# Two tiles instead of one between a head pair's projection and its turn into q and k, with one more tile of lead

## The chip, the core and the metric

The kernel runs on one core of one Trainium2 chip. The metric is the device time of one launch in microseconds (us), as the median of several runs. Four compute engines matter here: TensorE (PE, matrix products and transposes into PSUM), VectorE (DVE), ScalarE (ACT) and GpSimd (POOL). SyncE (SP) issues nearly all DMA transfers. Each engine takes its instructions in the order in which they were written into its own queue, and waits where an operand or a buffer is not ready.

## The reference

One block of a hybrid decoder, on a sequence of 2048 tokens of width 1024. The input is normalised (RMS), scaled and shifted by a conditioning vector, and multiplied by one matrix whose columns feed three mixers: A, a chunked gMLP with four groups of 64 columns; B, an mLSTM with four heads of 96; C, a stick-breaking attention with six heads of 64. The gated outputs are joined, projected, and added to the input. The change touches C alone:

```
q, k = rms_norm(q, g_q), rms_norm(k, g_k)          # over each head's 64 columns
for blk in range(S // 128):                        # 128 queries, all keys up to them
    z = (q_blk @ k^T) * 64 ** -0.5
    beta = sigmoid(z), 0 where key >= query        # strictly causal
    # a key's weight is beta there, times the product of (1 - beta) over
    # the keys between it and the query
    att = beta * reversed exclusive cumprod(1 - beta)
    out_blk = att @ v
```

## The kernel before

The 2048 tokens are 16 tiles of 128, worked on in three blocks of 5, 5 and 6 tiles (`BLOCKS`). Within a block the normalised, modulated input lies transposed in SBUF (`hT`), split into a coarse and a fine part; each projection is three matrix products for each of eight slices of the inner dimension, 24 matrix products for a tile (L297 to L299; `pc` is the projection of C, `pv`, `pb` and `pg` of B, `pa` of A). They go into a PSUM pool of three buffers, `pproj`.

The attention C runs in each block as three stages, one for each pair of heads (`p` = 0, 1, 2). For each tile of the pair, `c_proj` makes q, k and v, and `c_evac` takes them from PSUM in two parts. Part one (L351 to L362): ScalarE squares, VectorE sums (L353), GpSimd takes the power -1/2 (L354, L355), v is copied, and VectorE writes the normalised `qk` (L360), which is the last reader of the PSUM buffer. Part two, behind the `yield`, is the turning: four PE transposes `pq` (L366), two ACT copies (L369, L370), two VectorE operations into `Kst` (L371) and `Qst` (L373), and in blocks 0 and 1 two DMAs that keep k and v for later blocks.

The attention itself, `stick`, is a software pipeline of units (a tile, a head, up to four key tiles): products `z` (L401, L402), two sigmoids on ACT (L406, L407), a scan on VectorE (L414), a multiplication (L418) that goes by turns to VectorE and GpSimd, transposes `at` on PE (L429), ACT and VectorE splitting them into `aT` (L431, L432), and the products `av` (L444). A query tile ends with L448, L450 and two small products `py` (L460). `interleave` mixes these units by cost with a side stream: the rest of the pair's projection and then other projections as fillers, wrapped by `behind`.

`need` lets an attention unit of tile j start only once `ready` has reached j, which `evac_finish` sets when a tile's turning has been written. `lead` says how many tiles of the pair's projection are written ahead of the attention. The last stage of a block runs beside a short filler list, and then comes the tail: the projection `pv` of the block, into which the next block's input is mixed. `get_x` loads a tile, VectorE scales it (L149), GpSimd adds the shift (L150), and `hT_half` transposes it (L289) into a `pproj` buffer and splits it (ACT L290, VectorE L291).

All of this is the order in which the program is written. A list scheduler with priorities then places each engine's instructions, so what is written earlier in the text is a priority and not yet the order of a queue.

Of the kernel before, what the change touches and what calls it, by code (L numbers as in the profile page):

```python
# [33 lines left out]
def hybrid_block_kernel(ctx: ExitStack, tc: tile.TileContext, x, c, norm_g, w_ada, b_ada, w_in,  # L34
# [120 lines left out]
    def get_x(i, j):  # L155
        load_x(i, j % 2)
        rms_x(i)
        for hh in range(len(xtiles[i][0])):
            w = D // len(xtiles[i][0])
            mod_x(i, hh * w, (hh + 1) * w)  # L160
# [158 lines left out]
    pend = []  # L319
# [1 line left out]
    ready = [-1]  # L321

    def evac_finish():
        j, e = pend.pop()
        run(e)
        ready[0] = j

    def evac_later(e, j):

        next(e)  # L330
        if pend:
            evac_finish()
        pend.append((j, e))

    def behind(cp, rest):

        yield from cp
        for m, c in enumerate(rest):
            if m == 6 and pend:
                evac_finish()  # L340
            yield c
        if pend:
            evac_finish()

    def c_evac(b, t0, p, j, ps):
# [126 lines left out]
    def stick_cost(t0, nb):  # L472
        return sum(2 * ((i + 1) * (2 * P / 2.4 + 218) + 215) for i in range(t0, t0 + nb))
# [47 lines left out]
    def bg_proj(t0, nb, half):  # L521
        c0 = half * 192
        with prio(HIGH[0]):
            wt = weights(w_in[0], [(OFF["bo"] + c0, 192), (OFF["bz"] + c0, 192)])
        for j in range(nb):
            i = t0 + j
            ps = pproj.tile([P, 512], F32, tag="proj", name=f"pg{half}_{i}")
            yield from proj_tc(ps[:, :384], wt, j, 384)
            sg = t512(f"sgg{half}_{i}")
            nc.scalar.activation(sg[:, 0:384], ps[:, 0:384], AF.Sigmoid)  # L530
            g = t512(f"gg{half}_{i}")
            nc.vector.tensor_tensor(g[:, 0:192], ps[:, 192:384], sg[:, 192:384], ALU.mult)
            nc.gpsimd.tensor_tensor(sg[:, 0:192], sg[:, 0:192], hn_bc[:, c0:c0 + 192], ALU.mult)
            nc.gpsimd.tensor_tensor(g[:, 0:192], g[:, 0:192], sg[:, 0:192], ALU.mult)
            nc.sync.dma_start(gate_d[i * P:(i + 1) * P, c0:c0 + 192], g[:, 0:192])

    def cz_proj(t0, nb):
        with prio(HIGH[0]):
            wt = weights(w_in[0], [(OFF["cz"], 384)])
        for j in range(nb):  # L540
            i = t0 + j
            ps = pproj.tile([P, 512], F32, tag="proj", name=f"pcz{i}")
            yield from proj_tc(ps[:, :384], wt, j, 384)
            sg = t512(f"sgz{i}")
            nc.scalar.activation(sg[:, 0:384], ps[:, 0:384], AF.Sigmoid)
            nc.vector.tensor_tensor(sg[:, 0:384], ps[:, 0:384], sg[:, 0:384], ALU.mult)
            nc.sync.dma_start(gate_d[i * P:(i + 1) * P, 384:768], sg[:, 0:384])
# [181 lines left out]
    def gate_gemv():  # L729
        acc = tmp.tile([P, D], F32, tag="xt", name="gacc")  # L730
        for n in range(2):
            cs = slice(n * 512, (n + 1) * 512)
            for k in range(KT):
                st = stg_p.tile([P, 2, WMAX], F32, tag="st", name=f"stgate{n}_{k}").rearrange("p a f -> p (a f)")
                nc.sync.dma_start(st[:, 0:512], w_ada[0, k * P:(k + 1) * P, 2048 + n * 512:2560 + n * 512])
                if k == 0:
                    nc.vector.tensor_scalar(acc[:, cs], st[:, 0:512], c_act[:, 0:1], None, ALU.mult)
                else:
                    nc.vector.scalar_tensor_tensor(acc[:, cs], st[:, 0:512], c_act[:, k:k + 1], acc[:, cs],
                                                   ALU.mult, ALU.add)  # L740
                yield 0
            pg = pproj.tile([P, 512], F32, tag="proj", name=f"pgt{n}")
            nc.tensor.matmul(pg[0:1, :], lhsT=ones_sq[:, 0:1], rhs=acc[:, cs], start=True, stop=True)
            gr = t512(f"gate{n}")
            nc.sync.dma_start(gr[0:1, :], b_ada[:, 2048 + n * 512:2560 + n * 512])
            nc.vector.tensor_tensor(gr[0:1, :], pg[0:1, :], gr[0:1, :], ALU.add)
            nc.sync.dma_start(ga_d[:, cs], gr[0:1, :])
            yield 860

    def run(g):  # L750
        for _ in g:
            pass

    def chain(*gens):
        for g in gens:
            yield from g

    def mix(a, n, g):
        for m, c in enumerate(a):
            yield c  # L760
            if m % n == n - 1:
                yield next(g, 0)
        yield from g
# [75 lines left out]
    for b, nb in enumerate(BLOCKS):  # L839
        last = b == len(BLOCKS) - 1  # L840
        chunk = nb * KT * 3 * 384 / 2.4
        HIGH[0] = 0 if b == 0 else -4000
        fillers = [
            (chain(bqk_proj(t0, nb, 0), bqk_proj(t0, nb, 1), bg_proj(t0, nb, 0)), 3),
            (chain(bg_proj(t0, nb, 1), cz_proj(t0, nb), a_proj(t0, nb, 0)), 3),
            (a_proj(t0, nb, 1), 1),
        ]
        if b == 1:
            fillers[0] = (mix(fillers[0][0], 8, gate_gemv()), 3)
        if last:  # L850
            fillers[0] = (mix(fillers[0][0], 36, gating()), 3)
            fillers[1] = (mix(fillers[1][0], 14, first_chunk()), 3)
        for p in range(3):
            lead = min(nb, 2 + b)
            if p > 0:
                ready[0] = -1
                cp = c_proj(b, t0, nb, p)
                for _ in range(lead * KT + 1):
                    next(cp)
            cp_cost = 0 if b == 0 and p == 0 else (nb - lead) * KT * 3 * 384 / 2.4  # L860
            if b == 0 and p == 0:
                HIGH[0] = -400
            if p == 2 and not last:
                get_x(t0 + nb, 0)
                get_x(t0 + nb + 1, 1)
            interleave(stick(p, t0, nb), stick_cost(t0, nb), behind(cp, fillers[p][0]), cp_cost + fillers[p][1] * chunk)
        tail = bv_proj(t0, nb)
        if last:
            run(tail)
        else:  # L870
            t1, n1 = t0 + nb, BLOCKS[b + 1]
            ready[0] = -1
            cp = c_proj(b + 1, t1, n1, 0)
            lead = min(n1, 3 + b)
            for m, _ in enumerate(chain(tail, islice(cp, lead * KT + 1))):
                j = m // KT - 1
                if 0 <= j < n1 and m % KT in (1, 5):
                    if m % KT == 1 and j + 2 < n1:
                        get_x(t1 + j + 2, j + 2)
                    hT_half(t1 + j, j, m % KT // 4)  # L880
        t0 += nb
# [200 lines left out]
```

## Time and profile before

| | |
|---|---|
| Runs | 1473.59, 1475.47, 1473.66 us |
| Median | 1473.66 us |
| Profiled execution, its own time | 1471.23 us |
| Its span, first to last instruction | 1469.2 us |
| Mean granted TensorE clock | 0.988 |
| Busy share: PE, DVE, ACT, POOL | 95%, 69%, 46%, 44% |

The profiled execution is 2.43 us below the median of the runs. TensorE is busy for 1393.4 us of the span, so that some 76 us of it are idle time, and the rest is work whose length depends on the clock that is granted. In the rows below a bracket such as "[3.45 <-DVE hT L291]" means that the engine stood idle for 3.45 us before this instruction, and that what it waited for last was VectorE's write of `hT` at line 291.

### The profile page before, as it was taken

The page shows a single profiled execution, that of the slowest core. Times are in us where ns is not written, and L with a number is a line of the kernel's source. Part 1 is how long each engine was busy: PE and PEld are TensorE (multiplying, and loading weights), DVE is VectorE, ACT ScalarE, POOL GpSimd, SP SyncE. Part 2 cuts the span into 40 slices and gives each one's busy share as a digit, 9 for nine tenths or more (in the row PEclk, how much of TensorE's full clock was granted, in tenths as well). Part 3 has the DMA queues.
Part 4 walks back from the last instruction along what each step waited for, and adds up shares of the span by engine and source line. Part 5 has one row for each costly group of instructions (what it writes and reads, how often), then busy time and mean ns, then how long its engine had stood idle before and what let it go on. Part 6 is the DMA issues. An engine that isn't in the chain of part 4 may idle for free.

```text
span 1469.2 us, 24957 instructions
## 1 busy us (share of the span) xinstructions
PE 1393.4 (95%) x8468; PEld 1298.2 (88%) x8468; DVE 1018.8 (69%) x1778; ACT 676.5 (46%) x1656; POOL 647.6 (44%) x1140
## 2 busy tenths in 40 slices
PE   5999999898999999999999999999999978999998
PEld 3789999798999999988999899989999867888887
DVE  6797554676995666588799976778778788444543
ACT  3364454453554444346467655556455655111110
POOL 4473553743433432554343343434445337435442
PEclk8999999999999999999999999999999999999999
DMA  9866776666535533633433344303432435555541
GB/s 324 293 204 206 237 228 197 208 202 236 191 128 176 198 116 124 222 100 127 148 105 126 104 146 137 102 15 120 157 102 69 156 113 153 178 160 154 175 154 58
DMA packets 187103, 233.19 MB, mean 159 GB/s; under 512 B 22714, under 2 KB 160344, under 8 KB 186976
## 3 DMA queue, kind: packets, MB, share of 16 engines
q1 hardware_dynamic: 186752, 231.59, 48.5%
q8 instruction: 67, 1.10, 0.3%
q14 instruction: 60, 0.49, 0.1%
q0 software_dynamic: 224, 0.02, 0.0%
HBM read 159.24 MB, written 72.31 MB: 158 GB/s over the span
## 4 chain that ended last, share of the span: by engine, by line
PE 66%; DVE 15%; DMA 6%; issue 5%; POOL 4%; ACT 2%; SPq 1%; POOLq 0%; DVEq 0%; ACTq 0%
DVE bb L414 5%; PE av L444 5%; PE at L429 4%; PE pc L297 4%; PE pc L299 4%; PE pc L298 4%; PE po L995 4%; PE po L997 3%; PE po L996 3%; PE pg L297 3%; PE pg L298 3%; PE pg L299 3%; DMA st<-in_w_in_dram 2%; PE z L401 2%; PE z L402 2%
## 5 line engine op out<-in xcount | busy, mean ns | idle before, releaser
L414 DVE TENSOR_TENSOR_SCAN bb<-bb,bb 128x513 f32<-128x513 f32 x144 | 191.3, 1328 | 25.5 <-ACT bb L406 24.7
L418 POOL TENSOR_TENSOR be<-be,bb 128x512 f32<-128x512 f32 (+3 forms) x120 | 133.0, 1108 | 132.9 <-DVE bb L414 81.4
L432 DVE TENSOR_TENSOR aT<-at,aT 128x512 fp32r<-128x512 f32 (+3 forms) x240 | 142.3, 598 | 39.8 <-ACT aT L431 39.1
L406 ACT ACTIVATE bb<-z 128x512 f32<-128x512 f32 (+3 forms) x240 | 130.2, 543 | 80.5 <-PE z L402 61.2
L444 PE MATMUL av<-aT,Vst 128*128 128x256 f32 x816 | 148.7, 295 | 17.8 <-DVE aT L432 13.0
L431 ACT CAST aT<-at 128x512 fp32r<-128x512 f32 (+3 forms) x240 | 126.6, 529 | 83.8 <-PE at L429 82.7
L444 PEld LDWEIGHTS av<-aT,Vst 128*128 128x128 f32 x816 | 119.9, 189 | 30.1 <-DVE aT L432 21.0
L429 PE MATMUL at<-ident,be 128*128 128x128 f32 x816 | 132.7, 274 | 5.2 <-DVE aT L432 2.3
L297 PE MATMUL pc<-wr,hT 128*128 128x384 f32 (+1 forms) x384 | 134.8, 355 | 2.8 <-ACT hT L290 1.3
L299 PE MATMUL pc<-wr,hT 128*128 128x384 f32 (+1 forms) x384 | 134.7, 351 | 1.6 <-DVE hT L291 1.5
L298 PE MATMUL pc<-wr,hT 128*128 128x384 f32 (+1 forms) x384 | 133.4, 347 | 0.0
L407 ACT ACTIVATE be<-z 128x512 f32<-128x512 f32 (+3 forms) x240 | 131.7, 549 | 0.0
L429 PEld LDWEIGHTS at<-ident,be 128*128 128x128 f32 x816 | 99.2, 141 | 14.2 <-DVE aT L432 3.7
L995 PE MATMUL po<-wo,yT 128*128 128x512 f32 x256 | 104.9, 410 | 0.3 <-ACT yT L984 0.3
L414 DVE TENSOR_TENSOR_SCAN bb<-bb 128x129 f32<-128x129 f32 (+3 forms) x96 | 87.1, 911 | 23.3 <-POOL bb L409 16.8
L405 POOL MEMSET bb<- 128x1 f32 x240 | 23.5, 100 | 177.6 <-DVE bb L414 123.6
L996 PE MATMUL po<-wo,yT 128*128 128x512 f32 x256 | 101.6, 397 | 0.0
L997 PE MATMUL po<-wo,yT 128*128 128x512 f32 x256 | 101.4, 399 | 0.0
L487 PE MATMUL pb<-hT,wr 128*128 128x320 f32 (+1 forms) x288 | 93.2, 324 | 1.2 <-DMA wr<-w_d 1.2
L489 PE MATMUL pb<-hT,wr 128*128 128x320 f32 (+1 forms) x288 | 92.1, 323 | 1.8 <-DVE wr L191 1.3
L297 PE MATMUL pa<-wr,hT 128*128 128x384 f32 x256 | 88.2, 347 | 5.1 <-DVE qk L360 2.4
L401 PE MATMUL z<-Kst,Qst 128*128 128x512 f32 (+3 forms) x240 | 90.2, 385 | 2.4 <-DVE Kst L371 1.6
(273 smaller groups left out, 3900.3 us busy)
## 6 DMA issues: line engine op xcount, KB each, us to landing
wr<-w_d SPq DMA_DIRECT2D x160, 384.0 KB, 5.6
w_d<-wr SPq DMA_DIRECT2D x80, 384.0 KB, 3.4
wad<-in_w_ada_dram SPq DMA_DIRECT2D x8, 1024.0 KB, 6.7
xo<-in_x_dram SPq DMA_DIRECT2D x16, 512.0 KB, 3.8
out_dram<-o SPq DMA_DIRECT2D x31, 256.0 KB, 2.9
xt<-in_x_dram SPq DMA_DIRECT2D x15, 512.0 KB, 4.9
st<-in_w_in_dram SPq DMA_DIRECT2D x60, 128.0 KB, 3.4
wr<-w_d SPq DMA_DIRECT2D x16, 392.0 KB, 6.2
```

Of the source, the lines that this page charges most:

```text
L297: nc.tensor.matmul(ps, lhsT=hT[:, 0, k, cols], rhs=wt[k][:, 0, :W], start=k == 0, stop=False)
L298: nc.tensor.matmul(ps, lhsT=hT[:, 0, k, cols], rhs=wt[k][:, 1, :W], start=False, stop=False)
L299: nc.tensor.matmul(ps, lhsT=hT[:, 1, k, cols], rhs=wt[k][:, 0, :W], start=False, stop=k == KT - 1)
L407: nc.scalar.activation(be[:, :w], z[:, :w], AF.Sigmoid)
L414: nc.vector.tensor_tensor_scan(rev, rev, rev, carry.get((i, h), 1.0), ALU.mult, ALU.bypass)
L418: eng.tensor_tensor(be[:, :w], be[:, :w], bb[:, 1:w + 1], ALU.mult)
L429: nc.tensor.transpose(at[:, s, :], be[:, s * P:(s + 1) * P], ident)
L432: nc.vector.tensor_tensor(aT[:, :nb_, 1, :], at[:, :nb_, :], aT[:, :nb_, 0, :].bitcast(F32), ALU.subtract)
L444: nc.tensor.matmul(flat(av), lhsT=Vst[:, s0 + s, h, :], rhs=flat(aT[:, s]), start=(s0 + s == i), stop=(s0 + s == 0))
L995: nc.tensor.matmul(po, lhsT=yT[:, 0, k, :], rhs=wo[k][:, 0, cs], start=k == 0, stop=False)
L996: nc.tensor.matmul(po, lhsT=yT[:, 0, k, :], rhs=wo[k][:, 1, cs], start=False, stop=False)
L997: nc.tensor.matmul(po, lhsT=yT[:, 1, k, :], rhs=wo[k][:, 0, cs], start=False, stop=k == KT - 1)
```

## The change

`pend` holds the tiles whose projection has been evacuated but not turned. Before, it holds one: the turning of tile j is written right behind part one of tile j+1. Now it holds two: the turning of tile j is written behind part one of tile j+2. At the same time `lead` grows by one, as far as the block has tiles (`nb - 1` at most), so that at the first attention unit of a stage the same number of tiles has been turned as before, and one more has been projected. `behind` writes the two turnings that are left over at the fillers' steps 4 and 10, where the one stood at step 6.

```diff
     def evac_finish():
-        j, e = pend.pop()
+        j, e = pend.pop(0)
...
         next(e)
-        if pend:
+        pend.append((j, e))
+        if len(pend) > 2:
             evac_finish()
-        pend.append((j, e))
...
         for m, c in enumerate(rest):
-            if m == 6 and pend:
+            if m in (4, 10) and pend:
                 evac_finish()
             yield c
-        if pend:
+        while pend:
             evac_finish()
...
-            lead = min(nb, 2 + b)
+            lead = min(nb - 1, 3 + b)
...
-            lead = min(n1, 3 + b)
+            lead = min(n1 - 1, 4 + b)
```

No instruction is added or removed. What moves is seen in the queues. First VectorE's queue in the tail of block 0 (names with `_4_` belong to tile 4 of the attention, `xt` is the next block's input, `hT` its transposed form). Before:

```order
L149 SCALAR_TENSOR_TENSOR xt_4089<-xt_4089,ssq_4091,hscale 128x1024
L414 SCALAR_TENSOR_TENSOR bb_4_1_4_3799<-bb_4_1_4_3799 128x129
L432 TENSOR_TENSOR aT_4_0_4_3812<-at_4_0_4_3810,aT_4_0_4_3812 128x128
L418 TENSOR_TENSOR be_4_1_4_3800<-be_4_1_4_3800,bb_4_1_4_3799 128x128
L414 SCALAR_TENSOR_TENSOR bb_4_1_0_3836<-bb_4_1_0_3836,bb_4_1_4_3799 128x513
L291 TENSOR_TENSOR hT<-pt_0_4150,hT 128x4x128
```

and after the change, the same place:

```order
L418 TENSOR_TENSOR be_4_1_4_3809<-be_4_1_4_3809,bb_4_1_4_3808 128x128
L414 SCALAR_TENSOR_TENSOR bb_4_1_0_3862<-bb_4_1_0_3862,bb_4_1_4_3808 128x513
L432 TENSOR_TENSOR aT_4_0_4_3821<-at_4_0_4_3819,aT_4_0_4_3821 128x128
L450 TENSOR_TENSOR avt_3_1_3834<-av_3_1_3827,avs_3_1_3832 128x128
L149 SCALAR_TENSOR_TENSOR xt_4089<-xt_4089,ssq_4091,hscale 128x1024
L432 TENSOR_TENSOR aT_4_0_0_3880<-at_4_0_0_3875,aT_4_0_0_3880 128x4x128
L291 TENSOR_TENSOR hT<-pt_0_4150,hT 128x4x128
```

The multiplication L418 stood three places behind the scaling L149 and now stands ahead of it.

The same engine in the tail of block 1 (attention tiles 7 and 8), before:

```order
L149 SCALAR_TENSOR_TENSOR xt_8492<-xt_8492,ssq_8494,hscale 128x1024
L432 TENSOR_TENSOR aT_7_1_4_7959<-at_7_1_4_7954,aT_7_1_4_7959 128x4x128
L418 TENSOR_TENSOR be_8_0_0_8012<-be_8_0_0_8012,bb_8_0_0_8011 128x512
L450 TENSOR_TENSOR avt_7_0_7971<-av_7_0_7906,avs_7_0_7969 128x128
L432 TENSOR_TENSOR aT_7_1_0_7994<-at_7_1_0_7989,aT_7_1_0_7994 128x4x128
L291 TENSOR_TENSOR hT<-pt_0_8553,hT 128x4x128
```

and after:

```order
L432 TENSOR_TENSOR aT_7_1_4_7974<-at_7_1_4_7969,aT_7_1_4_7974 128x4x128
L418 TENSOR_TENSOR be_8_0_0_8038<-be_8_0_0_8038,bb_8_0_0_8037 128x512
L450 TENSOR_TENSOR avt_7_0_7983<-av_7_0_7938,avs_7_0_7981 128x128
L432 TENSOR_TENSOR aT_7_1_0_8023<-at_7_1_0_8018,aT_7_1_0_8023 128x4x128
L149 SCALAR_TENSOR_TENSOR xt_8492<-xt_8492,ssq_8494,hscale 128x1024
L291 TENSOR_TENSOR hT<-pt_0_8553,hT 128x4x128
L414 SCALAR_TENSOR_TENSOR bb_8_1_4_8102<-bb_8_1_4_8102,bb_8_1_8_8066 128x513
L432 TENSOR_TENSOR aT_8_0_8_8049<-at_8_0_8_8047,aT_8_0_8_8049 128x128
L418 TENSOR_TENSOR be_8_1_4_8103<-be_8_1_4_8103,bb_8_1_4_8102 128x512
```

L149 moved from two places ahead of one L418 to four places ahead of the next one.

Last, TensorE's queue in block 2, where the last filler product `pv` stands among the units of the last attention stage (`z_13_1_8` is tile 13, second head, key tiles 8 to 11). Before:

```order
L299 MATMUL pv_14742<-wr_7_14595,hT 128x384
L444 MATMUL av_13_0_13857<-aT_13_0_12_13822,Vst 128x256 x2
L460 MATMUL py_12_13860<-fold,avt_12_1_13834 128x64
L401 MATMUL z_13_1_0_13970<-Kst,Qst 128x512
L402 MATMUL z_13_1_0_13970<-Kst,Qst 128x512
```

and after:

```order
L299 MATMUL pv_14742<-wr_7_14595,hT 128x384
L401 MATMUL z_13_1_8_13927<-Kst,Qst 128x512
L402 MATMUL z_13_1_8_13927<-Kst,Qst 128x512
L444 MATMUL av_12_1_13765<-aT_12_1_0_13828,Vst 128x256 x4
L429 MATMUL at_13_0_8_13878<-ident,be_13_0_8_13817 128x128 x4
L460 MATMUL py_12_13889<-fold,avt_12_0_13739 128x64
L401 MATMUL z_13_1_4_13952<-Kst,Qst 128x512
L402 MATMUL z_13_1_4_13952<-Kst,Qst 128x512
```

The first unit behind the last filler was the third part of tile 13's second head (`z_13_1_0`) and is now its first full part (`z_13_1_8`), two units earlier in the attention.

## Rows read from the trace of the kernel before

**Rows 1.** Page, part 1: TensorE's busy time, share, instructions.

```profile
PE 1393.4 (95%) x8468; PEld 1298.2 (88%) x8468; DVE 1018.8 (69%) x1778; ACT 676.5 (46%) x1656; POOL 647.6 (44%) x1140
```

**Rows 2.** Waits of TensorE: line, releaser, total us, times, longest.

```profile
PE av L444 <- DVE aT L432: 13.0, 20, 1.2
PE av L444 <- DVE avt L450: 4.7, 7, 1.9
PE pv L297 <- DVE hT L291: 3.5, 1, 3.5
PE pa L297 <- DVE qk L360: 2.4, 2, 1.8
PE z L401 <- DVE Kst L371: 1.6, 1, 1.6
```

**Rows 3.** Timeline, tail of block 0: start, duration, engine, line [idle before].

```profile
332.73 2.42 POOL L150 TENSOR_TENSOR xt<-xt,hshift 128x1024 f32<-128x1024 f32 x1
333.11 2.18 DVE L418 TENSOR_TENSOR be<-be,bb 128x128 f32<-128x128 f32 x1
337.13 0.45 PE L297 MATMUL pv<-wr,hT 128*128 128x384 f32 x1 [3.45 <-DVE hT L291]
```

**Rows 4.** Timeline, tail of block 1, two places.

```profile
674.84 2.38 POOL L150 TENSOR_TENSOR xt<-xt,hshift 128x1024 f32<-128x1024 f32 x1 [1.46 <-DVE xt L149]
675.22 2.56 DVE L418 TENSOR_TENSOR be<-be,bb 128x512 f32<-128x512 f32 x1
678.03 1.34 PE L444 MATMUL av<-aT,Vst 128*128 128x256 f32 x8 [1.93 <-DVE avt L450]
...
697.17 2.02 DVE L418 TENSOR_TENSOR be<-be,bb 128x512 f32<-128x512 f32 x1
699.84 1.22 PE L444 MATMUL av<-aT,Vst 128*128 128x256 f32 x4 [1.10 <-DVE aT L432]
```

**Rows 5.** Line 418 on VectorE: count, duration in ns (least/median/most).

```profile
L418 DVE TENSOR_TENSOR be<-be,bb x120: 260/678/2556, 81.3 to 1201.3; 128x512 f32<-128x512 f32 x66, 128x128 f32<-128x128 f32 x18, 128x256 f32<-128x256 f32 x18, 128x384 f32<-128x384 f32 x18
```

**Rows 6.** Windows: length, busy (x) PE, PEld, DVE, ACT, POOL, granted clock, DMA.

```profile
336.00:340.00 4.00, 2.87 (x11) 2.88 (x12) 2.46 (x5) 1.48 (x3) 1.45 (x5) 0.75 0.22 89
340.00:344.00 4.00, 4.00 (x24) 3.98 (x24) 1.87 (x3) 0.98 (x5) 2.50 (x2) 0.83 0.19 65
680.00:684.00 4.00, 4.00 (x17) 3.99 (x17) 3.71 (x6) 2.49 (x5) 0.83 (x3) 0.66 0.13 42
700.00:704.00 4.00, 4.00 (x17) 4.00 (x18) 4.00 (x7) 2.26 (x4) 0.77 (x3) 0.60 1.05 398
```

**Rows 7.** Timeline, third stage of block 0.

```profile
269.95 0.56 DVE L191 TENSOR_TENSOR wr<-st,wr 128x384 fp32r<-128x384 f32 x1 [3.37 <-ACT wr L190]
271.16 0.66 PE L366 MATMUL pq<-ident,qk 128*128 128x128 f32 x4 [3.26 <-DVE qk L360]
```

**Rows 8.** Timeline, third stage of block 1.

```profile
618.96 3.24 POOL L150 TENSOR_TENSOR xt<-xt,hshift 128x1024 f32<-128x1024 f32 x1
622.16 1.01 POOL L355 TENSOR_TENSOR rr<-rr,neghalf 128x4 f32<-128x4 f32 x1
```

**Rows 9.** Page, part 5: busy, mean ns, then idle before.

```profile
L432 DVE TENSOR_TENSOR aT<-at,aT 128x512 fp32r<-128x512 f32 (+3 forms) x240 | 142.3, 598 | 39.8 <-ACT aT L431 39.1
L431 ACT CAST aT<-at 128x512 fp32r<-128x512 f32 (+3 forms) x240 | 126.6, 529 | 83.8 <-PE at L429 82.7
```

**Rows 10.** Windows: the last attention, ahead of and behind the last filler product.

```profile
1130.00:1160.90 30.90, 30.90 (x197) 30.07 (x196) 19.74 (x29) 16.80 (x37) 8.52 (x20) 1.00 0.08 29
1160.90:1196.60 35.70, 27.46 (x179) 21.72 (x177) 33.35 (x43) 26.26 (x56) 15.60 (x32) 1.00 0.70 242
```

**Rows 11.** Tile z on TensorE from 1160.8 to 1203 us: count, durations in ns.

```profile
L401 PE MATMUL z<-Kst,Qst x17: 396/477/501, 1161.2 to 1196.3; 128*128 128x512 f32 x15, 128*128 128x384 f32 x2
```

**Rows 12.** Timeline: two products of one projection, 18 products apart.

```profile
276.15 0.34 PE L299 MATMUL pc<-wr,hT 128*128 128x384 f32 x1
279.31 0.34 PE L299 MATMUL pc<-wr,hT 128*128 128x384 f32 x1
```

## The prediction, made before the changed kernel had run

> **What bounds the kernel now.** I read the page's first part first: TensorE is busy for 1393.4 of 1469.2 us [rows 1]. No instruction is added or removed, so its work stays, and what can move is its idle time, 75.8 us, and the stretches in which it ran at a lower granted clock. Next came TensorE's waits by line and releaser [rows 2]: apart from start-up and the final output projection, which the change doesn't touch, they are the attention waiting for VectorE (`av` for `aT` 13.0 us in 20 waits, `av` for `avt` 4.7 in 7), `pa` waiting for `qk` (2.4), `pv` for `hT` (3.5) and `z` for `Kst` (1.6); one more of 3.26 us, `pq` for `qk`, stands in block 0 [rows 7]. Then I looked for the places of the long ones in the timeline.
>
> Three of them have one cause, and all lie in the tails of blocks 0 and 1. GpSimd is adding the shift (L150) while VectorE takes up an attention multiplication (L418). In block 0's tail L150 runs from 332.73 for 2.42 us; L418 on 128x128 starts at 333.11 and takes 2.18, so it ends at 335.29, just behind L150's 335.15; `pv`, whose PSUM buffer is freed by the next L291 in VectorE's queue, starts after 3.45 us of idleness [rows 3]. In block 1's tail the same L418 takes 2.56 and 2.02 us, and `av` waits 1.93 and 1.10 us [rows 4]. The line alone takes 0.678 us in the median of 120, and 0.26 at the least [rows 5]. After each stall TensorE ran for a few us at a granted share below 1, so partly at 1.2 instead of 2.4 GHz: 0.75 and 0.83 in two windows of 4 us behind the first, 0.66 and 0.60 in one window behind the other two [rows 6]. A share g over 4 us of work costs 4 x (1 - g): 1.0 + 0.7 = 1.7 us, 1.4 and 1.6.
>
> **The change part by part.**
>
> *What the tails may give back.* In VectorE's new queue none of these three multiplications stands behind a scaling L149 that has just let a GpSimd addition go: in block 0 it stands ahead of L149, and so does the first of block 1, as the order shows; the second of block 1 (tile 9) too. Their stalls with the clock behind them are 3.45 + 1.7 = 5.15, 1.93 + 1.4 = 3.33, and 1.10 + 1.6 = 2.70 us, together 11.2 us.
>
> The price of such a meeting of L418 and L150 differs with what explains it. The rows show three multiplications that end 0.1 to 0.6 us behind the end of the addition, however many columns they have. The Trainium skill ("SBUF — State Buffer", section "Who interferes with whom") has a rule for this: VectorE's second pair of ports is shared with GpSimd and held exclusively, so that an operation with two SBUF inputs waits until the other engine's has finished; the trace agrees with 335.29 against 335.15. By that rule a meeting costs what is left of the addition, and an L149 moved behind one L418 may only have moved ahead of another. That is used below as a rival: in block 1 the next L418 behind the moved L149 is `be_8_1_4`, four places behind. Three instructions lie between them; at the mean of L432, 0.60 us [rows 9], they are 1.8 us, while L150 takes 2.4 [rows 3, 4]; the overlap is some 0.6 us at most.
>
> *What the turnings may give back.* `z` waits 1.6 us for `Kst` once, because its tile's turning was written late; TensorE now has a tile of projection more, about 24 products, between turning and use. The pitch of a product is (279.31 - 276.15)/18 = 0.176 us [rows 12], so 24 of them are 4.2 us, and this wait goes: 1.6. `pa` waits 2.4 us for `qk` in the third stage of block 1, since GpSimd does an addition of 3.24 us ahead of the power L355 [rows 8]; in the new order GpSimd's two power steps stand ahead of both additions, and the wait can go: 2.4. The long `pq` wait does not: `qk` is late there because VectorE sits 3.37 us in L191 behind ScalarE's copy of a weight [rows 7]. `pq` is moved away from it, but the next tile's first product needs that same `qk` to be done, since it is the last reader of one of three PSUM buffers. So 3.3 us stay with a new name: I count nothing for it.
>
> Together 11.2 + 1.6 + 2.4 = 15.2 us can go at most.
>
> *What of this comes back.* A stall on TensorE of 1 to 3 us was also slack for VectorE and ScalarE; without it they have less time ahead of the next unit. The 27 waits of `av` for VectorE are short and many (17.7 us in all [rows 2]), and they are set by how much TensorE work stands between `at` and `av`: ACT's and VectorE's splits take 0.53 + 0.60 us [rows 9], and where the order puts less than that plus the waiting in two queues between them, `av` waits. In the new order three more units have only 0.7 to 1.4 us of TensorE work there. No row shows these waits, as they don't exist yet: the bounds are 0 and 3 x 1.2 us (the longest `aT` wait in rows 2), 3.6. I take 1 us. For the returns of the large stalls the bounds are nothing and all of it; I take half, 7.6 us, between ends that no row decides.
>
> *What the later start costs.* In each stage the first attention unit stands one tile of projection, 4.2 us, later. Where fillers or a tail follow, the attention only mixes with other work. At the end of the last stage of block 2 there is none: from 1160.9 to 1196.6 us TensorE is busy for 27.46 of 35.70 us and VectorE for 33.35 [rows 10], with 17 `z` pairs in it [rows 11], so 2.1 us for each unit and 8.24/17 = 0.48 idle. By the new order the last `pv` product has two more units behind it (the order shows `z_13_1_8` where `z_13_1_0` stood): 2 x 0.48 = 1.0 us more. The ends are 0 (the scheduler already had this stage bound by TensorE) and the whole 4.2 us (VectorE bound from the start). I take 1.0.
>
> *The DMAs of a moved turning* (k and v to DRAM, in blocks 0 and 1) are written up to a tile later on SP's queue; they are read only a block later, and the weight loads behind them keep their order, so I cost them at nothing; if a weight load came late by them, the price would be of the size of the 3.37 us wait in rows 7.
>
> *Sum.* -7.6 + 1.0 + 1.0 = -5.6 us. On the profiled execution's own 1471.23 us that is 1465.6; it stood 2.43 below the median of the runs, so for the median 1473.66 - 5.6 = 1468.1 us.
>
> **The rivals.**
>
> *No change (the meetings only move).* Eleven additions L150 of 1024 columns remain, and all attention multiplications; as the ports' rule above would have it, each that meets an L150 waits. For it: the three meetings in the trace were placed by chance of the order, and the new order has two L418 within 3 us behind an L149. Against it: the estimate above puts such a meeting at the end of the addition, not at its start. If two of three meetings come back (7.5 of the 11.2 us), and half of the other 7.7 is kept, 3.9 - 2.0 = 1.9 us are gained: 1471.8 us, within 0.2%, which is 2.9 us and about what a measurement of this kernel can tell from no change.
>
> *Slower: the last attention is bound by VectorE from its start.* Then its end moves by the whole 4.2 us by which it starts later. For it: VectorE is busy for 93% of the stretch behind the last filler [rows 10]. Against it: in the 30.9 us ahead of that stretch TensorE has no idle time at all [rows 10], so it is TensorE's amount of work that paces there. This decides if the tails give back less than 1 us: 4.2 + 1.0 - 1.0, about 4.2 us slower, 1477.9 us.
>
> *All of it goes.* If no returns come: -15.2 + 2.0 = -13.2, 1460.5 us. For it: the stalls stand apart by tens of us, which leaves VectorE time to catch up between them. Against it: each stall is replaced by a queue in which VectorE still has the same work.
>
> *The change doesn't act,* the scheduler putting everything back: excluded, as the order shows other queues.
>
> **How the numbers follow.** My forecast (some 3 to 9 us gained) 0.48; the meetings move, 0.24; the slower case 0.17; all of it goes 0.11. The forecast's own range is 1464.5 to 1471. The range for 8 in 10 takes in the second rival and most of the two ends: 1460.5 to 1477.5. Faster by over 0.2% (below 1470.7): 0.11 + 0.42 of the forecast's 0.48 + 0.03 of the second = 0.56. Within: 0.06 + 0.19 + 0.01 = 0.26. Slower: 0.16 of the slower case + 0.02 of the second = 0.18.
>
> **What would show it.** In the profile after: no L418 on VectorE above 1.5 us in the two tails, no `pv` wait for `hT` of 3 us, and the granted clock at 1.00 in the windows of 60 us from 300 and 660 us; no `z` wait for `Kst`; `pa` for `qk` gone; a wait of about 3.3 us on `qk` still near 270 us, now before a `pc` product; 19 `z` pairs behind the last `pv` and 1 us more of idleness there. I am wrong if L418 still shows durations of 2 us beside L150, if `av`'s waits for VectorE grow beyond 24 us in sum (17.7 + half of the gain), or if the stretch behind the last filler grows by 4 us and TensorE's gain before it is less.

## The result, and the profile after

The changed kernel takes 1489.32 us (1487.66 to 1490.83, 4 runs) against 1474.27 us before (1473.59 to 1475.47): a ratio of 1.0103, 95% interval 1.0091 to 1.0116. It is 15 us slower, where 5.6 us were forecast as a gain. Its profiled execution took 1490.05 us over a span of 1488.3, which is 19.1 us more than the span before. Some 4 of these 19.1 us are the choice of the executions: the one profiled before lies 3.0 us below its median, the one after 0.7 above. TensorE's work is the same; its busy time and its waits by line are now (columns as in [rows 1, 2]):

```profile
PE 1404.1 (94%) x8468; PEld 1304.6 (88%) x8468; DVE 1027.0 (69%) x1778; ACT 677.9 (46%) x1656; POOL 654.6 (44%) x1140
```

```profile
PE av L444 <- DVE aT L432: 15.8, 20, 2.5
...
PE av L444 <- DVE avt L450: 6.6, 7, 1.4
...
PE at L429 <- DVE Qst L373: 3.6, 4, 1.5
PE z L401 <- ACT be L407: 3.1, 4, 1.9
...
PE pt L289 <- ACT vb L518: 2.6, 2, 2.0
...
PE z L401 <- DVE Kst L371: 1.6, 1, 1.6
```

Busy time rose by 10.7 us with the same 8468 products, and idle time by 8.4 (84.2 against 75.8). More busy time for the same products means a lower clock: the mean granted clock is 0.981 against 0.988. The wait of `pa` for `qk` is gone, and the wait of `z` for `Kst` has come back at another place with the same 1.6 us (at 646.60 instead of 658.34 us).

The span is best cut at landmarks that both kernels have: the first `pb` of the last block; the first `pc` of its second stage; the first `pc` of its third; the end of its last `pv`; the end of the last `av`; the end. Windows between these, before (length, then busy time and count of PE, PEld, DVE, ACT, POOL, then granted clock, DMA share, GB/s):

```profile
0.00:740.44 740.44, 693.49 (x4206) 659.19 (x4206) 515.23 (x931) 350.96 (x914) 339.47 (x636) 0.98 0.59 193
740.44:872.91 132.47, 129.66 (x825) 124.24 (x824) 119.95 (x196) 88.35 (x186) 55.81 (x116) 1.00 0.32 103
872.91:1045.02 172.11, 168.44 (x1073) 161.40 (x1072) 124.15 (x203) 92.40 (x215) 66.99 (x131) 1.00 0.33 109
1045.02:1161.01 115.99, 115.24 (x721) 111.35 (x721) 84.87 (x155) 59.70 (x152) 47.43 (x99) 1.00 0.29 92
1161.01:1208.56 47.55, 35.76 (x233) 28.24 (x233) 42.64 (x55) 31.58 (x66) 18.05 (x34) 1.00 0.53 183
1208.56:1469.20 260.64, 250.81 (x1419) 213.82 (x1417) 132.00 (x241) 53.48 (x126) 119.86 (x126) 0.98 0.48 147
```

and after:

```profile
0.00:741.02 741.02, 694.95 (x4197) 659.58 (x4198) 515.13 (x928) 350.53 (x909) 342.61 (x634) 0.98 0.59 193
741.02:878.61 137.59, 131.44 (x813) 123.53 (x813) 119.94 (x197) 89.19 (x187) 55.93 (x113) 0.99 0.30 97
878.61:1052.94 174.33, 169.24 (x1073) 162.24 (x1073) 124.23 (x201) 91.54 (x212) 66.32 (x132) 1.00 0.32 106
1052.94:1172.37 119.43, 115.95 (x726) 111.93 (x726) 86.72 (x155) 59.30 (x152) 49.67 (x97) 1.00 0.30 95
1172.37:1228.05 55.68, 43.05 (x247) 35.35 (x247) 48.91 (x61) 33.86 (x72) 19.26 (x40) 0.88 0.44 157
1228.05:1488.30 260.25, 249.46 (x1419) 212.00 (x1417) 132.03 (x241) 53.52 (x126) 120.77 (x126) 0.99 0.48 148
```

Subtracting line by line: blocks 0 and 1 +0.6 us, the last block's first stage +5.1, its second +2.2, its third up to the last `pv` +3.4, the stretch behind the last `pv` +8.1, the output phase -0.4: 19.0, the 19.1 to rounding. So blocks 0 and 1, on whose tails the forecast rested, moved nothing in sum, and the last block lost it all. The stretch behind the last `pv`, in which no filler product is left to run beside the attention, is called the uncovered end below.

### The profile page after: what moved, and what is told of

It reads as the page before. It is cut to its first block, busy times and chain, and to the rows that moved or that the text cites. A ratio compares the mean times of both kernels' runs of the same rounds, so it can differ in the third digit from the quotient of the medians.

```text
span 1488.3 us, 24976 instructions
## 1 busy us (share of the span) xinstructions
PE 1404.1 (94%) x8468; PEld 1304.6 (88%) x8468; DVE 1027.0 (69%) x1778; ACT 677.9 (46%) x1656; POOL 654.6 (44%) x1140
## 4 chain that ended last, share of the span: by engine, by line
PE 65%; DVE 17%; issue 5%; DMA 5%; ACT 4%; POOL 3%; SPq 1%; DVEq 0%; POOLq 0%; ACTq 0%
DVE bb L414 6%; PE av L444 4%; PE pc L297 4%; PE pc L299 4%; PE pc L298 4%; PE po L995 4%; PE po L996 4%; PE po L997 4%; PE at L429 4%; PE pg L298 3%; PE pg L299 3%; PE pg L297 3%; PE z L401 2%; PE z L402 2%; DVE aT L432 2%
## 5 line engine op out<-in xcount | busy, mean ns | idle before, releaser
L414 DVE TENSOR_TENSOR_SCAN bb<-bb,bb 128x513 f32<-128x513 f32 x144 | 195.6, 1358 | 21.4 <-ACT bb L406 19.6
L418 POOL TENSOR_TENSOR be<-be,bb 128x512 f32<-128x512 f32 (+3 forms) x120 | 132.7, 1106 | 132.0 <-DVE bb L414 69.3
L429 PE MATMUL at<-ident,be 128*128 128x128 f32 x816 | 135.6, 278 | 10.4 <-DVE Qst L373 3.6
L487 PE MATMUL pb<-hT,wr 128*128 128x320 f32 (+1 forms) x288 | 93.4, 326 | 1.8 <-DMA wr<-w_d 1.8
L489 PE MATMUL pb<-hT,wr 128*128 128x320 f32 (+1 forms) x288 | 92.5, 324 | 0.5 <-POOL bb L405 0.5
L488 PE MATMUL pb<-hT,wr 128*128 128x320 f32 (+1 forms) x288 | 92.8, 323 | 0.0
```

The lines of the kernel that those rows point to most:

```text
L414: nc.vector.tensor_tensor_scan(rev, rev, rev, carry.get((i, h), 1.0), ALU.mult, ALU.bypass)
L418: eng.tensor_tensor(be[:, :w], be[:, :w], bb[:, 1:w + 1], ALU.mult)
L429: nc.tensor.transpose(at[:, s, :], be[:, s * P:(s + 1) * P], ident)
```

## The experiments

Three theories stood at the start. L: the larger lead starts each attention late. T: the later turning makes `at` and `z` wait. S: any edit lays out all queues anew, and chance meetings decide. All runs below were timed in rounds against the kernel before, whose medians lay between 1473.0 and 1474.3 us; ratios are to it, with 95% intervals.

**The two halves of the change.** `a_turn_only` keeps the old leads; `b_lead_only` keeps the old turning:

```diff
-            lead = min(nb - 1, 3 + b)          # a: the changed kernel with the
+            lead = min(nb, 2 + b)              #    old leads (in the tail too)
...
-            lead = min(nb, 2 + b)              # b: the kernel before with the
+            lead = min(nb - 1, 3 + b)          #    new leads (in the tail too)
```

> Only the turning is two tiles behind (and the two left-over turnings at fillers' steps 4 and 10); the leads are those of before. Theory L (the lead: attention starts a tile of projection later in every stage and piles up where no filler is left) expects no loss: 1470 to 1478 us. Theory T (the turning: q and k of a tile come later, `at` and `z` wait for them, and their PSUM and SBUF buffers are held longer) expects most of the 15 us: 1483 to 1492 us. Theory S (the scheduler lays out every queue anew on any edit, and the sum of its chance meetings decides) expects something in between, with stalls at other places than in the changed kernel.

> Only the leads are larger by one; a tile is turned one tile behind as before. L expects most of the loss: 1483 to 1492 us, with some 19 z pairs behind the last pv product and the end of the last attention 5 us or more later than the last pv explains. T expects 1470 to 1478 us. S expects anything between 1470 and 1490, not adding up with the other half to 15 us.

Measured: a 1481.03 us (1.0048, 1.0033 to 1.0064), b 1491.62 us (1.0121, 1.0102 to 1.0140). The larger lead without the later turning loses more than the whole change, so T as the main cause falls. But a lies between the ranges of L and T, where S had put it, and the halves make 6.9 + 17.4 us where the whole makes 15.1, so they don't add up. In a the last block's first stage, 132.47 us before, becomes

```profile
737.26:881.02 143.76, 136.01 (x844) 127.97 (x844) 127.86 (x205) 95.08 (x198) 60.60 (x123) 0.99 0.28 94
```

Kernel c below has the same turning and, in the last block, the same leads as a, and takes 134.90 us there. So it is the old leads in blocks 0 and 1, together with the later turning, that cost a this stage. Its first `z` there stands behind 135 products of the stage's projection in a, behind 95 in the kernel before, 98 in c and 109 in the changed one (counted in the traces).

**The lead, block by block and stage by stage.** All four kernels are the changed one with other leads in the last block (b = 2; the first stage's lead is set in the tail of block 1):

```diff
-            lead = min(nb - 1, 3 + b)
+            lead = min(nb - 1, 3 + b) if b < 2 else 4              # c, h
+            lead = min(nb - 1, 3 + b) if b < 2 or p == 2 else 4    # g
+            lead = min(nb - 1, 3 + b) if b < 2 or p == 1 else 4    # m
...
-            lead = min(n1 - 1, 4 + b)
+            lead = min(n1 - 1, 4 + b) if b < 1 else 4              # c, g, m
```

> The changed kernel, with the old lead of 4 tiles in the three stages of the last block alone. L expects that at least half of the loss goes, since the fillerless end stands in that block: 1476 to 1483 us, with 17 z pairs behind the last pv. T expects no change against the changed kernel: 1486 to 1492 us. S expects a difference of several us in either direction, from blocks 0 and 1 too where their queues differ.

> The kernel with the old lead of 4 in the last block (1474.7 us), but with the new lead of 5 in that block's third stage. Theory L1 (only the stage that has no filler behind it pays for the later start) expects most of the 14.6 us here: 1484 to 1490 us. Theory L2 (each of the three stages of the last block pays for itself, since each mixes the same attention with a tile of products less) expects a third: 1477 to 1481 us. Theory U (what counts is how many attention units are left behind the last pv product: 17 here, 19 in the changed kernel) expects no loss: 1473 to 1477 us.

> The same with the new lead of 5 in the second stage of the last block only. L1 expects 1473 to 1477 us. L2 expects 1477 to 1481 us. U, with 20 units left behind the last pv product, expects a loss of the size of the changed kernel's: 1484 us or more.

> The same with the new lead of 5 in the first stage of the last block only (it is written in the tail of block 1). L1 expects 1473 to 1477 us. L2 expects 1477 to 1481 us. U, with 17 units behind the last pv product, expects 1473 to 1477 us.

| Lead 5 in the last block's | median us | ratio, interval |
|---|---|---|
| no stage (c) | 1474.70 | 1.0003, 0.9992 to 1.0015 |
| third stage (g) | 1474.79 | 1.0010, 0.9999 to 1.0021 |
| second stage (m) | 1485.93 | 1.0087, 1.0064 to 1.0110 |
| first stage (h) | 1479.36 | 1.0047, 1.0031 to 1.0063 |
| all three (the change) | 1489.32 | 1.0103, 1.0091 to 1.0116 |

Kernel c shows that the new turning and the new leads in blocks 0 and 1 together cost nothing that can be told apart. Of the 14.6 us between c and the change, the second stage's lead alone carries 11.2, the first's 4.7, the third's 0.1; they make 16.0, so these don't quite add up either. L1, my own reading, falls. U named the second and third rightly and the first wrongly; L2 has the first alone right. The loss of m is not in the second stage. Windows from the end of the last `pv` to the end of the last `av`, first in c, then in m:

```profile
1165.97:1213.64 47.67, 35.74 (x233) 28.24 (x233) 42.98 (x55) 31.60 (x66) 17.92 (x34) 1.00 0.53 183
```

```profile
1169.17:1226.35 57.18, 45.11 (x255) 37.66 (x255) 48.99 (x61) 35.19 (x74) 20.11 (x40) 0.85 0.43 153
```

TensorE's queue shows where the difference comes from. In the kernel before, in c and in g the third stage's first `z` stands among the products of that stage's last tile, `pc_15`; in m, in the change and in b it stands some 24 products later, among those of the next filler, `pa_10`. In g that is so although the third stage's own lead is 5: it starts when the second stage's attention runs out, and it is the second stage's lead that moves that point. The traces agree: from c to m the second stage's first `z` stays behind the same 130 products of its projection, and the third stage's comes 25 products later. What is late has less filler left, so that 20 units stand behind the last `pv` in m, and 17 in c and g.

**Lead in the other direction, and a step of the fillers.**

```diff
-            lead = min(nb, 2 + b)                       # i: before, last block
+            lead = min(nb, 2 + b) if b < 2 else 3       #    (in the tail too)
...
-            if m == 6 and pend:                         # d: before
+            if m == 8 and pend:
```

> The kernel before, with a lead of 3 instead of 4 in all three stages of the last block. If the loss comes from starting the attention of that block late, starting it earlier should not lose; L1 and L2 expect 1465 to 1475 us. U, with 18 units behind the last pv product instead of 17, expects about 1 to 3 us more than before: 1475 to 1478 us.

> The kernel before, with the one left-over turning written at the fillers' step 8 instead of 6; leads and depth as before. L and T expect nothing that matters: 1472 to 1477 us. S expects a move of 4 us or more in either direction, with stalls and half-clock stretches at other places than before.

Measured: i 1485.36 us (1.0085, 1.0068 to 1.0102), d 1476.38 us (1.0013, 0.9999 to 1.0028). The new layout of d alone is not told apart from nothing, and c and g, whose queues are new as well, lose nothing either; S as the cause of 15 us falls. Run i missed all three expectations: a smaller lead loses too, 12.1 us. Its first stage takes 144.34 us where 132.47 stood, with TensorE idle for 9.6 of them instead of 2.8. By the trace that stage's first `z` stands behind the same 95 products as before, but the second stage's comes 34 products sooner, so that the first stage's attention has 289 projection products beside it instead of 323. That this is what leaves TensorE idle there is a reading; it was not tried by itself.

**What paces the uncovered end.** In the last block's third stage all multiplications L418 go to GpSimd (n: before; o: the changed kernel):

```diff
-            eng = nc.gpsimd if len(st_count) % 2 else nc.vector
+            eng = nc.gpsimd if len(st_count) % 2 or (p == 2 and t0 + nb == NT) else nc.vector
```

> The kernel before, with all attention multiplications (L418) of the last block's third stage on GpSimd instead of every second one; all else as before. Theory V (the stretch behind the last pv product is paced by VectorE, which is busy for 42.6 of its 47.6 us) expects that some 8 multiplications of 0.68 us less on VectorE shorten that stretch by 3 to 6 us: 1468 to 1471 us. Theory K (each unit is a chain from engine to engine, in which GpSimd's 1.1 us stands for VectorE's 0.68) expects no gain: 1473 to 1478 us.

> The changed kernel with the same edit. Its stretch behind the last pv product is 55.7 us long, with VectorE busy for 48.9. V expects 4 to 7 us less than the changed kernel: 1482 to 1485 us. K expects 1488 us or more.

Measured: n 1479.52 us (1.0042, 1.0029 to 1.0054), o 1494.04 (1.0142, 1.0126 to 1.0158), both slower than without the edit. In n the stretch behind the last `pv` is

```profile
1170.07:1219.53 49.46, 37.60 (x233) 31.24 (x233) 39.34 (x46) 31.54 (x66) 33.45 (x43) 0.93 0.50 176
```

VectorE's work fell by 3.3 us (from 42.64) and the stretch grew by 1.9; in o it fell by 4.0 us (48.91 to 44.87) and the stretch by 1.1 (55.68 to 54.58). So V, which expected 3 to 7 us, falls: the stretch does not follow VectorE's amount of work. That fits K, the chain from engine to engine, but does not show it: the edit also puts GpSimd's 1.1 us in place of VectorE's 0.68 in that chain, and the granted clock was 0.93 there.

**More cover.** Kernels p (before) and q (the changed one) move a whole filler of the last block; s, the two r_before and the two r_after move 1, 2 or 3 of six tiles of another filler, whose weights are then loaded twice:

```diff
+            fillers[1] = (mix(chain(bg_proj(t0, nb, 1), cz_proj(t0, nb)), 14, first_chunk()), 2)   # p, q
+            fillers[2] = (chain(a_proj(t0, nb, 0), a_proj(t0, nb, 1)), 2)
...
+            n3 = nb - 1                       # or nb - 2, nb - 3: s, r
+            fillers[1] = (mix(chain(bg_proj(t0, nb, 1), cz_proj(t0, nb, range(n3)), a_proj(t0, nb, 0)), 14,
+                              first_chunk()), 2 + n3 / nb)
+            fillers[2] = (chain(cz_proj(t0, nb, range(n3, nb)), a_proj(t0, nb, 1)), 2 - n3 / nb)
```

> The kernel before, with one filler projection (the first half of A, 48 x 3 products, some 25 us of TensorE work) moved in the last block from the second stage to the third. The last attention then has products beside it to its end (no z behind the last pv product, where 17 were), and the second stage has some 51 us of them beside its attention instead of 69. The theory that products beside the attention are what covers its waits expects that most of the 11.8 us of idleness behind the last pv goes and that the second stage pays 4 to 8 us: 1464 to 1472 us. If that cover isn't the point, 1473 to 1478 us.

> The changed kernel with the same move. If its loss is cover taken from the last attention, as the stage-wise runs suggest, the 8 us that its stretch behind the last pv product is longer go with that stretch, so that it comes near the kernel above: at most 6 us slower than that. If its loss is waits of another kind, it stays 12 us or more slower than that.

Measured: p 1494.45 us (1.0145, 1.0128 to 1.0161), q 1500.96 (1.0194, 1.0168 to 1.0220). Both are far slower; p missed both of its expectations. In p's profile the last `av` does end earlier, at 1204.79 us against 1208.56, with no unit uncovered. But the output phase behind it takes 286.4 us instead of 260.6. TensorE's waits there, and the window behind the last `av`:

```profile
PE s L667 <- DMA qk<-qkT_d: 10.0, 1, 10.0
PE po L998 <- DVE yT L986: 5.9, 1, 5.9
PE k L672 <- DVE C L963: 5.1, 1, 5.1
```

```profile
1204.79:1240.00 35.21, 14.43 (x66) 11.86 (x65) 18.34 (x14) 13.74 (x29) 16.23 (x14) 0.57 0.76 256
```

The uncovered stretch is where the output phase's loads run (DMA share 0.53 there in the kernel before); without it they are waited for, and the clock falls. The two kernels differ by 6.5 us where the changed one and the one before differ by 15; at most 6 had been expected if the loss is cover taken from the last attention.

> The kernel with the new lead of 5 in the last block's second stage only (1485.9 us), and one of the six tiles of a filler projection (the gate of C, 24 products, 4.2 us of TensorE work) moved from that stage to the third; its weights are loaded a second time for it. The order now has the first z of the third stage 629 us into the side stream (633 without the move, 629 in the kernel before) and 17 units behind the last pv product (20 without, 17 before). Theory P (the loss is cover taken from the third stage, whose start hangs on the second stage's end) expects the 11 us to go: 1473 to 1479 us. Theory W (waits inside the second stage, or the late turning there) expects 1483 us or more.

> The changed kernel with one of six tiles of the gate projection of C moved from the second to the third stage of the last block. The order has the third stage's first z at 629 us of the side stream (633 in the changed kernel, 629 in the one before) and 15 units behind the last pv product (19; 17). P expects the 8 us of the longer stretch back, while the loss of the first stage's lead (4.6 us alone) stays: 1477 to 1482 us. Theory W (waits inside the stages) expects 1486 us or more.

> The changed kernel with three tiles moved; 11 units behind the last pv product, where the changed kernel has 19 and the kernel before 17. P expects at least the 8 us back by which that stretch was longer, and more: 1474 to 1482 us. W expects 1486 us or more.

> The changed kernel with the old lead of 4 in the last block's third stage alone, the reverse of g_last_stage_lead5. Theory P (the third stage starts when the second ends, whatever its own lead is) expects nothing back, or one unit's loss more, since the order has 20 units behind the last pv product: 1487 to 1493 us. The prediction's own reading (that stage's later start costs) expects 4 us or more back: 1485 us or less.

Kernel e is the changed one with the lead of 4 for `(b, p) == (2, 2)` alone. Measured: s 1472.09 us (0.9992, 0.9981 to 1.0003), so m's loss is gone whole with one tile of filler moved (m stood 12.7 us above the kernel before, s stands 0.9 below it). On the whole change one tile gives 1478.90 us (1.0031, 1.0015 to 1.0047), 10.4 us back; three give 1482.48 (1.0062, 1.0039 to 1.0085), 6.8 back; and the third stage's own lead (e) gives nothing: 1489.49 (1.0101, 1.0078 to 1.0125). Theory P (the loss is cover taken from the third stage, whose start hangs on the second stage's end) has e and the one tile in its ranges; s lies 0.9 us below its range, and the three tiles give 6.8 back where P had at least 8. Theory W is wrong in s and in both r_after, and the prediction's reading (4 us or more back) in e. The stretch behind the last `pv` in s and in the changed kernel with one tile moved:

```profile
1158.47:1206.04 47.57, 35.79 (x234) 28.30 (x233) 42.98 (x55) 31.58 (x66) 18.02 (x34) 1.00 0.54 183
```

```profile
1173.81:1217.55 43.74, 32.20 (x207) 25.21 (x207) 39.86 (x50) 27.72 (x58) 16.09 (x31) 1.00 0.59 198
```

Units behind the last `pv` and length of the stretch, over the profiles: 11 units 35.2 us (three tiles moved on the changed kernel); 13 units 40.8 (three tiles moved on the kernel before); 15 units 43.7; 17 units 47.6 (before, c, g, s alike); 19 units 55.7 (the change); 20 units 57.2 (m) and 55.8 (e). Divided, that is 2.8 to 3.2 us for each unit, but each stretch holds an end of 12 us or more behind its last `z`, in which no unit starts. Before, the first and the last `z` stand at 1161.2 and 1196.3 us [rows 11], so 35.1/16 = 2.2 us from unit to unit; in the changed kernel it is 41.8/18 = 2.3:

```profile
L401 PE MATMUL z<-Kst,Qst x19: 392/477/775, 1172.2 to 1214.0; 128*128 128x512 f32 x17, 128*128 128x384 f32 x2
```

The end behind the last `z`, before and after:

```profile
1196.30:1208.56 12.26, 8.71 (x59) 6.86 (x59) 9.70 (x13) 5.44 (x11) 2.45 (x2) 1.00 0.03 7
```

```profile
1214.00:1228.05 14.05, 10.96 (x60) 9.44 (x59) 10.10 (x13) 5.43 (x11) 2.46 (x2) 0.76 0.03 6
```

Of the 8.1 us by which the stretch grew, two more units at 2.2 us make 4.4, and the end is 1.8 longer at a lower granted clock; the rest, some 2, is the longer step from unit to unit.

> The kernel before, with two of those six tiles moved from the second to the third stage of the last block: 8.4 us more cover for the last attention, 16 units behind the last pv product. P expects a small gain or none, as the second stage gives up what the third gets: 1468 to 1475 us. W expects no effect: 1472 to 1476 us.

> The same with three tiles, 12.6 us, and 13 units behind the last pv product. P expects 4 units fewer at the uncovered pace, some 2 to 6 us gained: 1467 to 1472 us, unless the output phase, whose loads ran beside the uncovered stretch, then waits for them. W expects no effect.

The kernel before gains nothing from the same move: 1478.49 us (1.0038, 1.0022 to 1.0053) and 1476.27 (1.0022, 1.0010 to 1.0034), above P's range both times. With three tiles its stretch is 40.8 us for 13 units, 6.8 us shorter, and the second and third stage together are some 12 us longer. So cover given to the end is taken from the stages ahead, and what that costs there differs from kernel to kernel. No version was clearly faster than the kernel before.

## Why the prediction was wrong, point by point

**The tails: right in mechanism, mis-sized.** The meetings of L418 with L150 that stood in [rows 3, 4] are gone. The addition beside the third of them, which [rows 4] leave out, was in the kernel before

```profile
695.35 3.28 POOL L150 TENSOR_TENSOR xt<-xt,hshift 128x1024 f32<-128x1024 f32 x1 [1.40 <-DVE xt L149]
```

One new meeting stands in block 1's tail (L418 on 128x256, GpSimd's addition beside it):

```profile
690.30 3.29 POOL L150 TENSOR_TENSOR xt<-xt,hshift 128x1024 f32<-128x1024 f32 x1
...
691.91 1.96 DVE L418 TENSOR_TENSOR be<-be,bb 128x256 f32<-128x256 f32 x1
```

It is the rival "the meetings only move" at one place of three. That tail, from its first `pv` to the next block's first `pc`, took 50.2 us before (651.38 to 701.57) and takes 43.9 now (658.85 to 702.71): 6.3 us gained, where the two stalls with their clock were put at 6.0. The granted clock from 660 to 720 us is 1.00 (0.94 before). Block 0's tail gave back only 0.5 us (40.8 to 40.4) of 5.15. `pv`'s wait for `hT` is down to 1.1 us at most, but others stand there now, and the clock fell behind them as before:

```profile
336.67 0.33 PE L429 MATMUL at<-ident,be 128*128 128x128 f32 x1 [1.82 <-DVE aT L432]
...
353.48 0.66 PE L289 MATMUL pt<-ident,xt 128*128 128x128 f32 x4 [2.03 <-ACT vb L518]
```

```profile
338.00:342.00 4.00, 4.00 (x17) 4.00 (x17) 1.70 (x4) 2.10 (x4) 1.33 (x4) 0.63 0.23 87
```

Nearly all of block 1's gain was lost ahead of it: its third stage's first `pc` already came 5.8 us later (592.42, now 598.21).

More executions bear this out. Up to 720 us the engines' sequences of the kernel before stand also in i, n, p and the two r_before, and those of the changed kernel in c, e, g, h, m, o, q, s and the two r_after. Over these 6 and 11 profiles, in medians, block 0's tail takes 40.3 and 40.4 us, block 1's takes 48.7 and 43.9, and block 1's third stage begins at 592.9 and 596.8. The last block's first `pb`, up to which 5 and 6 of them still agree, stands at 740.8 and 740.9 us. It scatters from 740.2 to 746.8 and from 738.4 to 741.2, so a few us between two single profiles decide nothing there. The last block's first two stages scatter less: 132.47 and 172.11 us before and 132.45 and 171.20 in n, whose queues there are the same; 137.59 and 174.33 in the changed kernel and 137.63 and 174.42 in e. So of the 11.2 us block 1's tail alone gave back some 4.8, and the 7.6 that I counted came to nothing by the end of block 1: taking half was still too much, as kernel c shows in its time. What makes block 1's third stage begin later was not settled.

**The turnings and the short waits.** `pa`'s wait is gone as forecast, `z`'s 1.6 us is not. `av`'s waits for VectorE, for whose growth I took 1.0 us, grew from 17.7 to 22.4.

**The `pq` wait: right in size, wrong in name.** 3.24 us of it stay at 271.53 us, still ahead of `pq` and not of `pc`.

**The later start: the step that failed.** The 1.0 us that I took for it measured 14.6, the difference between c and the changed kernel. It rested on three things. First, each stage was to start one tile of projection, 24 products, later: in the last block's three stages the first `z` stands 14, 4 and 24 products later. Second, I charged only the last stage, as if its own lead set its start. Runs g and e show that its lead does nothing; the second stage's lead sets its start, by the end of its attention (m, s), and I had charged the second and the first stage nothing ("where fillers or a tail follow, the attention only mixes with other work"). Third, the price: the two more units behind the last `pv` were foreseen, the 19 `z` pairs are there, and TensorE's idleness in the stretch grew by 0.84 us (12.63 against 11.79), close to the 1.0 forecast. But I took idleness for the price, and that holds only if the stages that had lost a unit get shorter by the rest of it. They were longer too (5.1, 2.2 and 3.4 us), while the stretch grew by 8.1: two units at their whole 2.2 us and 3.7 more.

**The slower rival: right in sign and place, wrong in lever and bound.** It put the loss at the uncovered end, at most 4.2 us of it, and gave VectorE as the bound. The stretch alone grew by 8.1, and run n takes VectorE's work away without shortening it. Its point of decision ("if the tails give back less than 1 us") was met.

**What stays open.** Why the first stage's lead alone costs 4.7 us (in run h the second stage is longer, 176.75 us against 171.75 in c), why the halves don't add up, and what the pressed first stage waits for unit by unit were not settled. That filler moved to the end makes the loss good is shown by s and the moved tile on the whole change; the same move gains nothing on the kernel before, so how much cover is worth in general is not shown. The 2.2 us from unit to unit are measured, and the link of the chain that is longest was not tried apart from L418. How much of the 3.7 us is the lower clock is open: no profile has 19 units there at a granted 1.00; b has them at 0.94, in 54.0 us against 55.7 at 0.88.

## What to carry to other kernels

Before moving the start of a long chain of dependent units, ask what covers it until its end. A unit that loses its cover adds its whole pace there, and the idle time seen in that pace is its price only if the stages ahead get shorter by the rest; look whether they can. Where stages follow one another, the start of the last one can hang on the end of the one before and not on its own parameter: read its place from the queue in both kernels. And a stall removed in the middle can be worth nothing: here block 1's tail gave back 4.8 us, and the last block began no earlier.

## What the runs showed of the hardware

The same stall was followed by a drop of TensorE's clock in one execution and by none in another. In the kernel before and in i the order of block 0 is the same; `pq` waits 3.26 and 3.38 us there, and in the 6 us from its start the granted clock is, before and in i:

```profile
271.16:277.16 6.00, 6.00 (x37) 5.96 (x38) 4.46 (x8) 3.18 (x11) 4.71 (x7) 1.00 0.43 143
```

```profile
269.74:275.74 6.00, 6.00 (x22) 6.00 (x23) 4.46 (x8) 2.00 (x6) 4.72 (x7) 0.54 0.36 125
```

In those 6 us TensorE issued 37 and 22 instructions. A price for the clock that is read off one profile, as the 1.4 to 1.7 us behind each stall in the prediction, therefore holds only for that execution. Another pair shows the same: p has the sequence before and the same two long L418 in block 1's tail, and its granted clock from 660 to 720 us is 1.00 where it was 0.94.

What a lower clock costs depends on where it falls. Behind the last `pv` TensorE's sequence is the same in c, g and a, with 47.67 us at a granted 1.00 in c. In g and a it is

```profile
1162.22:1209.84 47.62, 36.86 (x234) 29.83 (x233) 43.18 (x55) 31.49 (x66) 18.10 (x35) 0.96 0.53 183
```

```profile
1170.83:1219.24 48.41, 37.06 (x234) 29.80 (x233) 42.88 (x55) 31.69 (x66) 17.94 (x34) 0.96 0.51 180
```

In g, where the low clock lies among the units, nothing is lost; in a, where it lies behind the last `z`, 0.7 us are. The sequence of m (57.18 us at 0.85) stands also in e, 1.4 us shorter:

```profile
1172.04:1227.82 55.78, 43.59 (x255) 36.40 (x255) 48.67 (x61) 35.01 (x74) 19.80 (x40) 0.88 0.44 156
```
